# Moving a pool of streamed tiles to the other end of SBUF, in a decoder trunk on one core

## The chip, the cores and the metric

The kernel runs on one NeuronCore of a Trainium2 chip, as one launch. The metric is the device time of an execution in microseconds (us); three executions of the kernel before the change took 1943.15, 1944.34 and 1944.63 us, median 1944.34 us.

## The reference, cut to what matters

A trunk of two residual layers works on 256 tokens of width 1024. Each layer has a mixer and then an expert network with 16384 single-neuron experts. Every token picks, in 8 heads, 16 experts each, out of 128 x 128 product keys:

```python
def peer_ffn(h, w_q, sub_keys, u, v):
    ...
    def one_chunk(args):
        hc, ec, gc = args
        act = jax.nn.gelu(jnp.einsum('td,ted->te', hc, u[ec]).astype(f32), approximate=False)
        return jnp.einsum('te,ted->td', (gc * act).astype(v.dtype), v[ec])
```

`u` and `v` are 16384 x 1024 tables in float32.

## The kernel before, in words

The kernel gathers nothing. For each layer it streams both tables whole, in slabs of 128 experts (128 slabs of `u`, 128 of `v`, 512 KB each, two layers), computes every expert for every token, and masks with the gates.

A float32 product is made of three products of a reduced type: each operand is split into a rounded part `hi` and a rest `lo`. The helper `split` (L131) does it: a copy on ScalarE (ACT) writes `hi`, a subtraction on VectorE (DVE) writes `lo`. On TensorE (PE) each matrix product has a *stationary* operand, loaded by LDWEIGHTS (PEld in the profile), and a *moving* operand that streams past it.

**First product** (`u_pair`, `u_slab`). A slab of `uT` lands in a tile `raw`, is split into `hi` and `lo` (two buffers each), and 24 matmuls follow: 16 on L626 with `hi` stationary, 8 on L628 with `lo` stationary. The moving operand is always `hT`, the normalized activations (256 columns, one token a column). The first half of a layer's slabs runs beside the choice of the experts (`choose`, on DVE, in an order fixed by `in_order("DVE")`); in the second half, after every two slabs, `g_batch` makes gates of eight tokens with 16 small matmuls (L649).

**Second product** (`v_pair`, `v_acts`, `v_slab`). For two slabs the masked activations `act` are split into `whi` and `wlo` (two buffers each). A slab of `v` lands in `raw` and is split into `hi` and `lo`. Then 12 matmuls on L783 follow, with `whi` or `wlo` stationary and `hi` or `lo` moving, 512 columns each. The last six slabs of a layer run at L736.

**Where the tiles lie.** A pool takes a piece of SBUF of the same address range in all 128 partitions: from the bottom upward, or with `side="right"` from the top downward. A pool opened later lies behind the ones that are open on its side. `base` and `h` (with `hT`) are opened first at the bottom; then `st`, with `raw` (3 buffers), `hi` and `lo` (2 each); above it come the pools of the stage. At the top lie the weights of the projections (pool `wp`, with tiles that are also tagged `whi` and `wlo`) and later some activations. `whi` and `wlo` of the second product are in the pool `oh`, at the bottom above `st`.

The other user of such matmuls that the text needs is `proj_t` and `proj_n` (lines L135 to L137 by way of `mm3`), which multiply `hT` (or another tile of activations) by weights from the pool `wp`: in `proj_t` the weights are stationary, in `proj_n` they move.

Of the kernel before, what the change touches and what calls it, by code (L numbers as in the profile page):

```python
# [10 lines left out]
F32R = mybir.dt.float32r  # L11
# [8 lines left out]
P = 128  # L20
D = 1024
KD = D // P
S = 256
# [4 lines left out]
NK = 128  # L28
# [39 lines left out]
class Trunk:  # L68
# [222 lines left out]
    def tail(self, products, add, nxt, tmp):  # L291


        def run(g):
            for _ in g:
                pass
        run(products(0, 0))
        run(products(0, 1))
        run(add(0, 0))
        run(add(0, 1))  # L300
        nxt.norm(0)
        run(products(1, 0))
        p = products(1, 1)
        next(p)
        squares = add(1, 0)
        next(squares)
        nxt.turn(0)
        run(p)
        nxt.make(0, tmp, squares)
        run(add(1, 1))  # L310
# [351 lines left out]
    def peer(self, layer, e, first, right, early, middle, after, nxt, ss):  # L662

        st = self.st
        nb = S // GB
        left = ExitStack()
        dp = left.enter_context(self.pool(f"dst{layer}"))
        dst = self.t(dp, [P, 4, S], HF)  # L670
        with self.pool(f"topk{layer}") as tk:
            self.topk_consts(tk)
            mods = self.mods_in(tk, 3, *early)
            sc = [self.t(tk, [P, 16, NK]) for _ in range(TT)]
            with self.pool(f"q{layer}") as qp:
                self.queries(qp, layer, e, first, sc, mods)
            right.close()
            act0 = self.act_tiles(right.enter_context(self.pool(f"act0_{layer}", side="right")))
            chosen = self.choose(tk, sc, dst)
            with self.in_order("DVE"):  # L680
                for q in range(0, HALF, 2):
                    self.u_pair(st, layer, q, e.hT, act0, chosen)
                    if q % 4:
                        next(mods, None)
                for c in (chosen, mods):
                    for _ in c:
                        pass
        mods = self.mods_in(left.enter_context(self.pool(f"mm{layer}")), 2, *middle) if middle else iter(())
        oh = left.enter_context(self.pool(f"oh{layer}"))
        a1 = left.enter_context(self.pool(f"act1_{layer}"))  # L690
        act1 = self.act_tiles(a1)
        self.iota_t = self.t(oh, [P, NK, 2], HF)
        self.nc.gpsimd.iota(self.iota_t, pattern=[[1, NK], [0, 2]], base=0, channel_multiplier=0,
                            allow_small_or_imprecise_dtypes=True)
        done = 0
        for q in range(0, HALF, 2):
            self.u_pair(st, layer, HALF + q, e.hT, act1)
            if q % 4:
                next(mods, None)
            while done < nb and done * (HALF - 4) < nb * (q + 2):  # L700
                self.g_batch(oh, dst, act0, 0, done * GB)
                done += 1
        for _ in mods:
            pass
        accs = [[self.ps("o") for _ in range(2)] for _ in range(TT)]
        done = 0
        for q in range(0, HALF, 2):
            self.v_pair(oh, layer, q, act0, accs, q == 0)
            while q % 4 == 2 and done < nb and done * (HALF - 4) < nb * (q + 2):
                self.g_batch(oh, dst, act1, 1, done * GB)  # L710
                done += 1
        right.close()
        mods, ready = after()
        late = self.t(a1, [P, 4, 2, D], F32R, tag="act")
        nv = 6
        vs = []
        for q in range(0, HALF - nv, 2):
            self.v_pair(oh, layer, HALF + q, act1, accs, False)
            if q % 4:
                next(mods, None)  # L720
            if 34 <= q < 50 and q % 4 == 2:
                n = len(vs)
                vs.append(self.v_slab(layer, NK - nv + n, late[:, n, 0], late[:, n, 1]))
        for _ in mods:
            pass
        self.row_of(self.gate, self.modc[layer][:, 40:48])
        self.begin_order()
        ready()
        ws = [self.v_acts(oh, NK - nv + q, act1, *(("ohA", "ohA") if q == 2 else ("whi", "wlo"))) for q in (0, 2, 4)]
        vs += [self.v_slab(layer, NK - 2 + n, *self.v_parts()) for n in range(2)]  # L730

        def products(i, c):
            for m in range(0, nv, 2):
                for a, b in ((0, 0), (1, 0), (0, 1)):
                    for n in (m, m + 1):
                        self.nc.tensor.matmul(accs[i][c], ws[n // 2][a][:, n % 2, i * P:(i + 1) * P],  # L736
                                              vs[n][b][:, c * 512:(c + 1) * 512], start=False,
                                              stop=n == nv - 1 and b == 1)
                if not m:
                    yield  # L740

        def add(i, c):
            yield from self.add_gated(lambda: self.t(oh, [P, 256], tag="ohB", bufs=2), self.gate, i, c, accs[i][c], ss)
            nxt.added(i, c)
        self.tail(products, add, nxt, lambda: self.t(oh, [P, 512], tag="ohG", bufs=2))
        left.close()
# [22 lines left out]
        return [self.t(self.st, [P, D], F32R, tag=t, bufs=2) for t in ("hi", "lo")]  # L769

    def v_acts(self, pool, i2, act, *tags):
        hi, lo = (self.t(pool, [P, 2, S], F32R, tag=t, bufs=2) for t in tags or ("whi", "wlo"))
        self.split(hi, lo, self.act_of(act, i2))
        return hi, lo

# [865 lines left out]
    def run(self, out):  # L1641
        nc = self.nc
        self.hp = self.ctx.enter_context(self.pool("h"))
        self.st = self.ctx.enter_context(self.pool("st"))
        right, late = ExitStack(), ExitStack()
        self.order = ExitStack()
        start = ExitStack()
# [243 lines left out]
```

## Time and profile before

| what | value |
|---|---|
| median of three executions | 1944.34 us (1943.15 to 1944.63) |
| the profiled execution | 1942.01 us |
| its span, first to last instruction | 1940.2 us |
| PE busy | 1908.1 us, 98% of the span |
| DVE busy | 1534.9 us, 79% |
| ACT busy | 952.7 us, 49% |
| first product (L626, L628) | 4096 + 2048 matmuls |
| second product (L783) | 2928 matmuls |

The times that the text works out refer to the profiled execution, which lies 2.3 us under the median. A matmul's own duration in the profile is its way through the array; matmuls overlap, so that the distance from one start to the next is what a stream of them costs. That distance is read from a timeline: the difference of two starts, divided by the matmuls between them.

### The profile page before, as it was taken

The page shows a single profiled execution, that of the slowest core. Times are in us where ns is not written, and L with a number is a line of the kernel's source. Part 1 is how long each engine was busy: PE and PEld are TensorE (multiplying, and loading weights), DVE is VectorE, ACT ScalarE, POOL GpSimd, SP SyncE. Part 2 cuts the span into 40 slices and gives each one's busy share as a digit, 9 for nine tenths or more (in the row PEclk, how much of TensorE's full clock was granted, in tenths as well). Part 3 has the DMA queues.
Part 4 walks back from the last instruction along what each step waited for, and adds up shares of the span by engine and source line. Part 5 has one row for each costly group of instructions (what it writes and reads, how often), then busy time and mean ns, then how long its engine had stood idle before and what let it go on. Part 6 is the DMA issues. An engine that isn't in the chain of part 4 may idle for free.

```text
span 1940.2 us, 36008 instructions
## 1 busy us (share of the span) xinstructions
PE 1908.1 (98%) x14368; PEld 1753.0 (90%) x14368; DVE 1534.9 (79%) x3265; ACT 952.7 (49%) x1309; POOL 49.9 (3%) x131
## 2 busy tenths in 40 slices
PE   6999999999999999999999999999999999999998
PEld 6999999999999888888889899999999988888886
DVE  7879699989977789877657668898777778985565
ACT  3866545454344444445546664545444444444453
POOL 7000000000000000000000000000000000000000
PEclk9999999999999999999999999999999999999999
DMA  7557485558645555589743454555545555556673
GB/s 319 177 172 250 187 275 179 185 187 291 229 164 167 172 175 174 178 286 331 229 129 115 163 218 169 183 187 178 171 164 169 168 174 175 173 176 204 192 224 106
DMA packets 97080, 376.67 MB, mean 194 GB/s; under 512 B 11920, under 2 KB 12176, under 8 KB 90256
## 3 DMA queue, kind: packets, MB, share of 16 engines
q1 hardware_dynamic: 96912, 374.37, 57.4%
q8 instruction: 112, 1.84, 0.4%
q14 instruction: 56, 0.46, 0.1%
HBM read 373.28 MB, written 1.05 MB: 193 GB/s over the span
## 4 chain that ended last, share of the span: by engine, by line
PE 88%; DVE 4%; DMA 3%; ACT 2%; issue 1%; SPq 0%; ACTq 0%; DVEq 0%
PE ps L783 31%; PE ps L626 26%; PE ps L628 13%; PE ps L649 3%; PE ps L135 3%; PE ps L136 3%; PE ps L137 3%; DMA raw<-in_v_dram 2%; PE ps L736 1%; PE ps L323 1%; DVE wlo L131 1%; PE ps L1207 1%; DMA wraw<-in_w_dram 1%; PE ps L946 1%; PE ps L456 1%
## 5 line engine op out<-in xcount | busy, mean ns | idle before, releaser
L131 ACT CAST hi<-raw 128x1024 fp32r<-128x1024 f32 x508 | 533.6, 1051 | 772.6 <-PE ps L626 385.4
L131 DVE TENSOR_TENSOR lo<-raw,hi 128x1024 fp32r<-128x1024 f32 x508 | 619.8, 1221 | 260.7 <-ACT hi L131 256.7
L626 PE MATMUL ps<-hT,hi 128*128 128x256 f32 x4096 | 538.3, 284 | 0.0
L626 PEld LDWEIGHTS ps<-hT,hi 128*128 128x128 f32 x4096 | 509.0, 192 | 0.0
L628 PE MATMUL ps<-hT,lo 128*128 128x256 f32 x2048 | 287.2, 283 | 0.0
L783 PE MATMUL ps<-hi,whi 128*128 128x512 f32 x976 | 266.4, 394 | 2.0 <-ACT hi L131 1.9
L628 PEld LDWEIGHTS ps<-hT,lo 128*128 128x128 f32 x2048 | 264.2, 192 | 0.0
L783 PE MATMUL ps<-hi,wlo 128*128 128x512 f32 x976 | 261.3, 389 | 0.0
L783 PE MATMUL ps<-lo,whi 128*128 128x512 f32 x976 | 261.2, 389 | 0.0
L783 PEld LDWEIGHTS ps<-hi,wlo 128*128 128x128 f32 x976 | 183.2, 188 | 38.8
L783 PEld LDWEIGHTS ps<-lo,whi 128*128 128x128 f32 x976 | 183.1, 188 | 38.9 <-DVE lo L131 0.2
L783 PEld LDWEIGHTS ps<-hi,whi 128*128 128x128 f32 x976 | 180.1, 188 | 39.3 <-ACT hi L131 4.5
L131 DVE TENSOR_TENSOR wlo<-wraw,whi 128x1024 fp32r<-128x1024 f32 (+1 forms) x84 | 98.7, 1200 | 41.0 <-ACT whi L131 41.0
L131 ACT CAST whi<-wraw 128x1024 fp32r<-128x1024 f32 (+1 forms) x84 | 83.7, 1031 | 30.7 <-PE ps L137 9.3
L645 DVE TENSOR_TENSOR ohG<-ohB,t 128x512 f16<-128x512 f16 x256 | 98.6, 416 | 0.0
L135 PE MATMUL ps<-hT,whi 128*128 128x256 f32 x288 | 84.0, 292 | 7.7 <-ACT hT L246 7.1
L639 DVE TENSOR_TENSOR ohA<-t,t 128x1024 f16<-128x1024 f16 x128 | 87.3, 682 | 0.0
L136 PE MATMUL ps<-hT,whi 128*128 128x256 f32 x288 | 82.1, 285 | 0.2 <-DVE hT L250 0.2
L137 PE MATMUL ps<-hT,wlo 128*128 128x256 f32 x288 | 82.2, 286 | 0.0
L649 PE MATMUL ps<-ohG,ohA 128*128 128x64 f16 x2048 | 78.6, 193 | 0.0
L649 PEld LDWEIGHTS <-ohA 128*128 128x128 f16 x2048 | 67.0, 97 | 12.1 <-issue 8.5
L353 DVE SCALAR_TENSOR_TENSOR t<-t 128x1024 f32<-128x1024 f32 x56 | 67.4, 1219 | 12.6 <-DMA t<-in_modT_dram 9.5
(480 smaller groups left out, 2254.6 us busy)
## 6 DMA issues: line engine op xcount, KB each, us to landing
raw<-in_uT_dram SPq DMA_DIRECT2D x256, 512.0 KB, 3.3
raw<-in_v_dram SPq DMA_DIRECT2D x256, 512.0 KB, 3.8
t<-in_modT_dram SPq DMA_DIRECT2D x56, 512.0 KB, 5.3
wraw<-in_w_dram SPq DMA_DIRECT2D x13, 1024.0 KB, 5.9
raw<-in_modT_dram SPq DMA_DIRECT2D x24, 512.0 KB, 4.4
wraw<-in_wq_dram SPq DMA_DIRECT2D x12, 1024.0 KB, 5.9
mw<-in_mod_dram SPq DMA_DIRECT2D x8, 1024.0 KB, 13.8
wraw<-in_w0start_dram SPq DMA_DIRECT2D x4, 1024.0 KB, 12.0
```

Source lines behind the costliest of these rows:

```text
L131: return self.nc.scalar.copy(hi, src), self.nc.vector.tensor_sub(lo, src, hi.bitcast(F32))
L135: mm(out, l[0], r[0], start=start, stop=False)
L136: mm(out, l[0], r[1], start=False, stop=False)
L137: mm(out, l[1], r[0], start=False, stop=stop)
L323: mm(ps[g][:, i], e.hT[:, s, k, sl], w[:, b, k, :], start=s + k + b == 0, stop=s == 1 and n == KD - 1)
L353: self.nc.vector.scalar_tensor_tensor(w, w, 1.0, row, op0=OP.mult, op1=OP.mult, accum_out=self.modc[layer][:, c:c + 1])
L626: mm(pair, hi[:, k], hT[:, s, k], start=k == 0 and s == 0, stop=False)
L628: mm(pair, lo[:, k], hT[:, 0, k], start=False, stop=k == KD - 1)
L639: nc.vector.tensor_tensor(A, self.iota_t[:, None].to_broadcast(full), pairs(0, full), op=OP.is_equal)
L645: nc.vector.tensor_tensor(B[:, j], b0, pairs(2 + j, part), op=OP.mult)
L649: nc.tensor.matmul(ps[:, t], A[:, t // 2, :, t % 2], B[:, j, t // 2, :, t % 2], start=j == 0, stop=j == 1)
L783: self.nc.tensor.matmul(acc[i][c], w[a][:, j, i * P:(i + 1) * P], v[b][:, c * 512:(c + 1) * 512], start=first and j + a + b == 0, stop=False)
```

## The change

The pool `st` is opened at the top of SBUF (`side="right"`) instead of the bottom. The activations' parts of the second product, `whi` and `wlo`, leave the pool `oh` and go into `st` under the tags `vwh` and `vwl`; only one pair of the last six slabs keeps its place in `oh` (the tag `ohA`).

```diff
-        ws = [self.v_acts(oh, NK - nv + q, act1, *(("ohA", "ohA") if q == 2 else ("whi", "wlo"))) for q in (0, 2, 4)]
+        ws = [self.v_acts(oh, NK - nv + q, act1, *(("ohA", "ohA") if q == 2 else ())) for q in (0, 2, 4)]
...
     def v_acts(self, pool, i2, act, *tags):
-        hi, lo = (self.t(pool, [P, 2, S], F32R, tag=t, bufs=2) for t in tags or ("whi", "wlo"))
+        hi, lo = (self.t(pool if tags else self.st, [P, 2, S], F32R, tag=t, bufs=2) for t in tags or ("vwh", "vwl"))
         self.split(hi, lo, self.act_of(act, i2))
         return hi, lo
...
         self.hp = self.ctx.enter_context(self.pool("h"))
-        self.st = self.ctx.enter_context(self.pool("st"))
+        self.st = self.ctx.enter_context(self.pool("st", side="right"))
```

The instructions, their order on every engine, and the semaphores and counts that each waits for are the same in both programs. What differs is a name here and there and the addresses. On ACT, at the change from the first to the second product of layer 0, the difference reads as follows (`hi` is a slab's high part, `act` the masked activations, the number a buffer's):

```order
 L131 CAST hi_8249<-raw_8247 128x1024
 L766 ACTIVATE t_5489<-ps_8126 128x512
-L131 CAST whi_8347<-act_3027 128x512
-L131 CAST whi_8387<-act_3027 128x512
+L131 CAST vwh_8347<-act_3027 128x512
+L131 CAST vwh_8387<-act_3027 128x512
 L131 CAST hi_8281<-raw_8279 128x1024
 L131 CAST hi_8311<-raw_8309 128x1024
```

Nothing has moved: the same two casts stand at the same place, with another tag. SP, which issues the transfers, has no difference at all.

The first byte of some tiles in each partition, as the allocation of the two programs gives it, with its remainder by 128 bytes in brackets:

| tile | role | before | after |
|---|---|---|---|
| `hT` | moves in the first product | 13984 (32) | 13984 (32) |
| `hi` (two buffers) | stationary in the first product, moves in the second | 50848, 54944 (32) | 212960, 217056 (96) |
| `lo` (two buffers) | the same | 42656, 46752 (32) | 204768, 208864 (96) |
| `whi`/`vwh`, layer 0 | stationary in the second product | 84128, 86176 (32) | 221152, 223200 (96) |
| `wlo`/`vwl`, layer 0 | the same | 88224, 90272 (32) | 225248, 227296 (96) |
| `whi`, `wlo` of the projections | pool `wp` | 180192 to 229343 (96) | 143328 to 192479 (96) |
| `qkT` of the first mixer | stationary there | 93856 (32) | 65184 (32) |
| `qn` of the second mixer | stationary there | 83136 (64) | 54464 (64) |

All pools that stay at the bottom lie 28672 bytes lower after the change, all others at the top 36864 bytes lower; both are multiples of 128, so their remainders stay. Only the tiles of `st`, and with them `vwh` and `vwl`, have another remainder.

## Rows read from the trace of the kernel before

**Rows 1.** The page: busy time, and the chain that ended last.

```profile
PE 1908.1 (98%) x14368; PEld 1753.0 (90%) x14368; DVE 1534.9 (79%) x3265; ACT 952.7 (49%) x1309; POOL 49.9 (3%) x131
...
PE 88%; DVE 4%; DMA 3%; ACT 2%; issue 1%; SPq 0%; ACTq 0%; DVEq 0%
```

**Rows 2.** Groups of instructions: line, engine, names, shapes, count | busy us, mean ns | idle.

```profile
L626 PE MATMUL ps<-hT,hi 128*128 128x256 f32 x4096 | 538.3, 284 | 0.0
...
L628 PE MATMUL ps<-hT,lo 128*128 128x256 f32 x2048 | 287.2, 283 | 0.0
L783 PE MATMUL ps<-hi,whi 128*128 128x512 f32 x976 | 266.4, 394 | 2.0 <-ACT hi L131 1.9
```

**Rows 3.** PE's timeline, first product: start us, us, line, operation, count.

```profile
382.59 2.08 PE L626 MATMUL ps<-hT,hi 128*128 128x256 f32 x16
384.51 1.12 PE L628 MATMUL ps<-hT,lo 128*128 128x256 f32 x8
385.47 2.08 PE L626 MATMUL ps<-hT,hi 128*128 128x256 f32 x16
387.39 1.12 PE L628 MATMUL ps<-hT,lo 128*128 128x256 f32 x8
388.35 2.08 PE L626 MATMUL ps<-hT,hi 128*128 128x256 f32 x16
```

**Rows 4.** PE's timeline, projections with stationary weights: 36 matmuls between the rows.

```profile
240.92 0.28 PE L135 MATMUL ps<-hT,whi 128*128 128x256 f32 x1
...
245.00 0.28 PE L135 MATMUL ps<-hT,whi 128*128 128x256 f32 x1
```

**Rows 5.** The same, 20 us earlier: 27 matmuls between the rows.

```profile
219.81 0.28 PE L135 MATMUL ps<-hT,whi 128*128 128x256 f32 x1
...
222.99 0.28 PE L135 MATMUL ps<-hT,whi 128*128 128x256 f32 x1
```

**Rows 6.** Three stretches: length, PE, PEld, DVE, ACT, POOL busy, granted clock, DMA.

```profile
219.80:223.00 3.20, 3.20 (x30) 3.20 (x29) 2.45 (x3) 2.71 (x4) 0.00 (x0) 1.00 1.01 410
240.90:245.00 4.10, 4.10 (x38) 4.10 (x37) 2.80 (x3) 2.21 (x3) 0.00 (x0) 1.00 0.96 384
382.00:389.00 7.00, 7.00 (x61) 7.00 (x60) 6.16 (x28) 3.85 (x5) 0.00 (x0) 1.00 0.58 186
```

**Rows 7.** PE's timeline, second product of layer 1: 20 matmuls between the rows.

```profile
1880.43 1.07 PE L783 MATMUL ps<-hi,whi 128*128 128x512 f32 x4
...
1884.96 1.07 PE L783 MATMUL ps<-lo,whi 128*128 128x512 f32 x4
```

**Rows 8.** PE's timeline, moving weights over `qkT`: 18 matmuls between the rows.

```profile
184.27 0.39 PE L135 MATMUL ps<-whi,qkT 128*128 128x512 f32 x1
...
188.39 0.39 PE L135 MATMUL ps<-whi,qkT 128*128 128x512 f32 x1
```

**Rows 9.** PE's timeline, moving weights over `qn`: 18 matmuls between the rows.

```profile
1109.20 0.39 PE L135 MATMUL ps<-whi,qn 128*128 128x512 f32 x1
...
1113.40 0.39 PE L135 MATMUL ps<-whi,qn 128*128 128x512 f32 x1
```

**Rows 10.** Stretches of the first product: length, PE, PEld, DVE, ACT, POOL busy, clock, DMA.

```profile
262.00:300.00 38.00, 38.00 (x319) 38.00 (x318) 37.41 (x145) 18.73 (x23) 0.00 (x0) 1.00 0.70 233
300.00:347.00 47.00, 47.00 (x394) 47.00 (x394) 43.24 (x130) 23.74 (x28) 1.53 (x1) 1.00 0.56 183
349.00:400.00 51.00, 51.00 (x428) 51.00 (x427) 48.54 (x223) 22.80 (x26) 0.00 (x0) 1.00 0.54 180
...
454.00:500.00 46.00, 46.00 (x464) 45.70 (x463) 46.00 (x86) 18.73 (x22) 0.00 (x0) 1.00 0.83 281
...
1264.00:1300.00 36.00, 36.00 (x302) 36.00 (x302) 34.32 (x143) 16.69 (x19) 0.00 (x0) 1.00 0.54 180
...
1368.00:1450.00 82.00, 82.00 (x832) 81.44 (x831) 62.72 (x110) 33.87 (x39) 0.00 (x0) 1.00 0.50 166
```

**Rows 11.** PE's timeline, first product's second half: one round of two slabs and gates.

```profile
497.28 2.16 PE L626 MATMUL ps<-hT,hi 128*128 128x256 f32 x16
...
503.61 1.56 PE L626 MATMUL ps<-hT,hi 128*128 128x256 f32 x11
```

**Rows 12.** Waits between 262 and 652 us: who waited for whom, us, times, longest.

```profile
ACT hi L131 <- PE ps L626: 184.9, 111, 2.4
...
DVE lo L131 <- ACT hi L131: 43.7, 41, 1.9
ACT hi L131 <- DMA raw<-in_uT_dram: 14.4, 7, 2.5
```

## The prediction, as it was recorded before the result was known

> **What bounds the kernel now.** I read the page first: PE is busy for 98% of the span, and 88% of the chain that ended last is PE [rows 1]. The reader is to see there that neither a wait nor a transfer is to be won; time can only come from the rate at which PE runs its stream. The groups of instructions give the size of the two streams: 6144 matmuls of 256 columns in the first product, none with idle time before it, and 2928 of 512 columns in the second (976 for each of three products of parts, of which one row stands for all) [rows 2]. Then I looked at PE's timeline for the distance from start to start. In the first product two slabs take 388.35 - 382.59 = 5.76 us for 48 matmuls, 120.0 ns each [rows 3]. In the projections, where `hT` moves over weights of the pool `wp`, a matmul of the same shape follows the last after 4.08 / 36 = 113.3 ns [rows 4]; a little earlier, with the same operands from the same kind of tiles, after 3.18 / 27 = 117.8 ns [rows 5]. The granted clock is 1.00 in each of these stretches [rows 6], the full 2.4 GHz, so the three spacings are not the clock's.
>
> What differs between [rows 3] and [rows 4] is the place of the stationary operand. `hT` has remainder 32 by 128 bytes in both. In [rows 3] `hi` and `lo` also have remainder 32, and lie at the bottom like `hT`; in [rows 4, 5] the weights have remainder 96, and lie at the top. The change gives the first product the placement of [rows 4, 5].
>
> **The change, part by part.** No instruction, wait or transfer is added, removed or moved, and no queue is passed by anything, so every term is a count times a difference of spacings.
>
> *First product.* 6144 matmuls. If they run like [rows 4], each saves 120.0 - 113.3 = 6.67 ns: 41.0 us. If they run like [rows 5], 120.0 - 117.8 = 2.2 ns: 13.5 us. I take [rows 4]: a spacing settles within some matmuls after a break in the stream and then stays, and the last projections before the first product, which begins right behind them, run at that of [rows 4]. Both values stay for the range.
>
> *What is late next.* DVE makes every `lo`. It waits for ACT, and ACT for PE to give a buffer back [rows 12]; so today PE paces it. With PE at 113.3 / 120.0 = 94.4% of its time per slab, DVE must not need more. In 262 to 300 us it needs 37.41 us where PE would take 35.9: 1.5 us are lost. In 349 to 400 it needs 48.54 against 48.2: 0.4 us. In 1264 to 1300, 34.32 against 34.0: 0.3 us [rows 10]. From 454 to 500 DVE is busy without a pause; a round of 48 matmuls takes 503.61 - 497.28 = 6.33 us there [rows 11], so 46 us hold some 350 of them, whose 2.3 us are all lost. In the other stretches, such as 300 to 347 (43.24 against 44.4) or 1368 to 1450 (62.72 of 82), DVE has room [rows 10]. Together 4.5 us. At the spacing of [rows 5] PE would need 98% of its time, and DVE hardly costs anything. Transfers: 14.4 us of ACT's waits are for slabs not yet landed [rows 12]; PE waits for none of it now, and at 5% more speed I leave it at nothing; if that cover goes, the few longest (up to 2.5 us each, 7 in all) are the price, which the range takes in.
>
> *Second product.* 2928 matmuls at 4.53 / 20 = 226.5 ns [rows 7]. Here both operands move together, from remainder 32 and the bottom to remainder 96 and the top. No row has both operands at the top, or both at remainder 96, so I bound it. Above: weights of remainder 96 moving over a stationary tile at the bottom take 4.12 / 18 = 228.9 ns over `qkT` [rows 8] and 4.20 / 18 = 233.3 ns over `qn` [rows 9]: +2.4 to +6.8 ns, 7 to 20 us slower. Below: if a high place alone were what helps, the 6.67 ns of [rows 4] against [rows 3], 20 us faster. I take zero, because the relation of the two operands, equal remainders and the same end, is that of [rows 7].
>
> *The rest.* `first_queries` also puts weights into `hi` and `lo`, and the last six slabs mix both places; some hundred matmuls with a few ns each, in both directions: nothing. The pools that only slide keep their remainders and their end.
>
> Sum: 41.0 - 4.5 = 36.5 us off the profiled execution's 1942.0 us gives 1905.5; the median stands 2.3 us above that execution, hence **1908 us**.
>
> **A rule that speaks against it.** The rows show three spacings for one shape and one clock. The Trainium skill, page "SBUF — State Buffer", section "SBUF: two separate sides", says that contention arises only at the port pair that GpSimd and VectorE share, or at the transfer side, and that TensorE never waits on anyone; page "TensorE: Matmul & The Clock Gate", part 2, adds that loading the next weights takes no read bandwidth from the running matmul. By these the place of a tile would cost nothing and the sum would be 0, with the time at 1944. The trace agrees badly: [rows 3] and [rows 4] differ by 6.67 ns with nothing else changed that I can name.
>
> **The rivals.**
> 1. *The slower of the two spacings.* The first product settles at that of [rows 5]. For it: the same kinds of tiles ran at both. Against it: [rows 4] are the nearer in time to the first product. 1944.3 - 13.5 = 1931 us.
> 2. *The place decides nothing.* The 120 ns come from how the first product is fed (ACT and DVE write `hi` and `lo` while PE reads), not from addresses. For it: [rows 4, 5] differ with the same tiles, so something besides place acts. Against it: the first three stretches of [rows 10] have 119 ns of PE's time per matmul alike (38.00 / 319, 47.00 / 394, 51.00 / 428, a matmul at either edge counted in), with DVE busy for 98, 92 and 95% of them. 1944 us. (The two pages of the Trainium skill named above would have this one.)
> 3. *The moving operand's own place decides, and a high one is slow* (the slower side). `hT` does not move, so the first product keeps 120 ns; in the second `hi` and `lo` now move from remainder 96 like the weights of [rows 8, 9]. For it: those rows are the slowest of the 512-column kind. Against it: [rows 3, 4] have the same `hT`. Its price is 7 us at 228.9 ns and 20 us at 233.3: 1951 to 1964 us. With the first product unchanged it decides as soon as the second goes over 226.5 by 1.3 ns (3.9 us over 2928 matmuls).
>
> **How the numbers follow.** Forecast 65%, with 1902 to 1918 of its own (from no loss on DVE, 1903, to some stretches at the spacing of [rows 5]); rival 1 20%; rival 2 8%; rival 3 7%. About 0.2% (3.9 us) is what a measurement of this kernel can tell from no change. Faster: 65 + 20 = 0.85; same 0.08; slower 0.07. The range must leave out no more than 2 in 10: from 1902 to 1932 it holds the forecast and rival 1 (0.85, less a little for their own edges), and part of the case in which the first product gains in full and the second loses up to 20 us.
>
> **What would show it.** In the profile after, PE's timeline of the first product should read 2.72 us for 24 matmuls where it now reads 2.88, and the duration of one matmul on L626 should fall from 283 or 284 ns to about 276; L783 should keep its spacing of 226.5 ns. The span of each first product should shrink by some 20 us in layer 1 and 16 in layer 0, where DVE's stretches without a pause lie, and waits of PE for `lo` should appear in those. Wrong it is if L626 keeps 120 ns, if L783 goes above 228 ns, or if PE's new waits for `lo` or for landed slabs go well beyond 5 us.

## The result, and the profile after

The changed kernel takes **1913.42 us**, the median of four executions (1911.78 to 1916.04); the kernel before, in four executions, takes 1944.49 us. The ratio is 0.9843, 95% interval 0.9826 to 0.986. The change is faster, as forecast, and lies 5 us above the predicted 1908 us and inside the range. The profiled execution went from 1942.01 to 1913.79 us: 28.2 us, where the sum said 36.5.

The page after, busy time and the chain that ended last; the lines answer to [rows 1]:

```profile
PE 1875.2 (98%) x14368; PEld 1716.0 (90%) x14368; DVE 1532.6 (80%) x3265; ACT 951.4 (50%) x1309; POOL 51.4 (3%) x131
...
PE 77%; DVE 10%; DMA 7%; ACT 4%; issue 2%; SPq 0%; ACTq 0%; DVEq 0%
```

The same 14368 matmuls keep PE busy for 33 us less. In the chain PE has given 11% of the span to the others, DVE (6%) and the transfers (4%) above all: PE still bounds the kernel, but no longer alone. The groups of instructions (busy us, mean ns of one | idle before), which answer to [rows 2]:

```profile
L626 PE MATMUL ps<-hT,hi 128*128 128x256 f32 x4096 | 513.1, 278 | 2.0 <-ACT hi L131 2.0
...
L628 PE MATMUL ps<-hT,lo 128*128 128x256 f32 x2048 | 275.7, 277 | 1.3 <-DVE lo L131 1.2
L783 PE MATMUL ps<-hi,vwh 128*128 128x512 f32 x976 | 266.5, 394 | 2.9 <-ACT hi L131 2.6
```

The gain is in the first two rows: a matmul of the first product falls from 284 and 283 ns to 278 and 277, L783 stays at 394, and small idle times stand behind the bars where [rows 2] has 0.0 for the first product. PE's timeline in the first product (start us, us, engine, line, operation, count), as in [rows 3]:

```profile
382.38 1.98 PE L626 MATMUL ps<-hT,hi 128*128 128x256 f32 x16
384.19 1.07 PE L628 MATMUL ps<-hT,lo 128*128 128x256 f32 x8
385.10 1.98 PE L626 MATMUL ps<-hT,hi 128*128 128x256 f32 x16
```

24 matmuls take 385.10 - 382.38 = 2.72 us, 113.3 ns each, the predicted figure to the digit. The second product, as in [rows 7]:

```profile
1879.83 1.07 PE L783 MATMUL ps<-hi,vwh 128*128 128x512 f32 x4
...
1884.37 1.07 PE L783 MATMUL ps<-lo,vwh 128*128 128x512 f32 x4
```

20 matmuls in 4.54 us: 227 ns, unchanged.

To add up a whole product, the distance from the start of each of its matmuls to the start of PE's next one was taken. A distance of at most 25 ns above 256 or 512 columns at 2.4 GHz (106.7 or 213.3 ns) counts as part of a stream, whose mean is its *spacing*; what longer distances have beyond this mean is the *loss at breaks*. "Span" is from the first start to the last end.

| | before | after |
|---|---|---|
| first product, spacing of 6144 matmuls | 119.98 ns | 113.71 ns |
| first product, loss at breaks | 5.3 us | 12.1 us |
| second product (L783), spacing | 227.3 ns | 227.2 ns |
| second product, loss at breaks | 6.8 us | 9.7 us |
| span of the first product, layer 0 and 1 | 387.5, 387.5 us | 374.7, 368.9 us |
| span of the second product, layer 0 and 1 | 352.8, 351.1 us | 356.0, 350.7 us |

The faster spacing gives 6144 x 6.27 = 38.5 us; new breaks take back 12.1 - 5.3 = 6.8 us in the first product and 9.7 - 6.8 = 2.9 us in the second: 28.8 us, against 28.2 measured. Nearly all of the new breaks are in layer 0 (6.4 of the 6.8 us), whose first product won 12.8 us where layer 1's won 18.6; forecast were 16 and 20.

The breaks in the trace. Stretches of the changed kernel (length, then PE, PEld, DVE, ACT and POOL busy, granted clock, DMA share, GB/s), as in [rows 10]:

```profile
262.00:300.00 38.00, 38.00 (x338) 38.00 (x337) 37.72 (x147) 20.09 (x25) 0.00 (x0) 1.00 0.71 235
300.00:347.00 47.00, 46.76 (x407) 46.24 (x406) 44.99 (x141) 24.40 (x29) 1.53 (x1) 1.00 0.56 189
454.00:500.00 46.00, 44.76 (x462) 43.68 (x461) 46.00 (x84) 18.53 (x21) 0.00 (x0) 1.00 0.81 278
```

In 454 to 500 DVE has no pause and PE stands still for 1.24 us, mostly in waits for `lo` of up to 0.5 us, as predicted. It gets through 462 matmuls there, where [rows 10] has 464, so the faster spacing wins nothing in this stretch: counted from start to start, the loss at breaks is 3.0 us against 0.6 before. PE's idle time shows only a part of such a loss. In 262 to 300 PE loses nothing (338 matmuls for 319), where 1.5 us were predicted. In 300 to 347, where room was predicted, it is idle for 0.24 us and loses 1.2 us from start to start. The largest single break is elsewhere, on ACT (ACT's timeline, then PE's next matmul, with the idle time and its releaser):

```profile
433.25 1.28 ACT L349 ACT_TABLE_LOAD   x1 [3.81 <-DMA t<-in_cond_dram]
434.55 1.06 ACT L349 ACTIVATE t<-t 128x1024 f32<-128x1024 f32 x1
435.51 1.03 ACT L131 CAST hi<-raw 128x1024 fp32r<-128x1024 f32 x1
```

```profile
436.59 0.61 PE L626 MATMUL ps<-hT,hi 128*128 128x256 f32 x3 [1.89 <-ACT hi L131]
```

At the start of layer 0's second half `mods_in` makes its row of conditions on ACT. ACT waits 3.81 us for the row, and the next slab's `hi` is queued behind it. Before, the same wait was 1.5 us and PE had no idle time for it; now the break costs PE 2.1 us from start to start.

### The profile page after: what moved, and what is told of

The parts are those of the page before. It is cut to its first block, busy times and chain, and to the rows that moved or that the text cites. A ratio compares the mean times of both kernels' runs of the same rounds, so it can differ in the third digit from the quotient of the medians.

```text
span 1912.0 us, 36008 instructions
## 1 busy us (share of the span) xinstructions
PE 1875.2 (98%) x14368; PEld 1716.0 (90%) x14368; DVE 1532.6 (80%) x3265; ACT 951.4 (50%) x1309; POOL 51.4 (3%) x131
## 4 chain that ended last, share of the span: by engine, by line
PE 77%; DVE 10%; DMA 7%; ACT 4%; issue 2%; SPq 0%; ACTq 0%; DVEq 0%
PE ps L783 26%; PE ps L626 21%; PE ps L628 11%; DMA raw<-in_v_dram 4%; DVE lo L131 3%; PE ps L649 3%; PE ps L135 3%; PE ps L137 3%; PE ps L136 3%; DMA t<-in_modT_dram 2%; PE ps L736 1%; ACT hi L131 1%; DVE t L353 1%; PE ps L323 1%; PE ps L1207 1%
## 5 line engine op out<-in xcount | busy, mean ns | idle before, releaser
L131 ACT CAST hi<-raw 128x1024 fp32r<-128x1024 f32 x508 | 534.4, 1054 | 741.8 <-PE ps L626 301.1
L131 DVE TENSOR_TENSOR lo<-raw,hi 128x1024 fp32r<-128x1024 f32 x508 | 619.2, 1221 | 233.6 <-ACT hi L131 231.0
L626 PE MATMUL ps<-hT,hi 128*128 128x256 f32 x4096 | 513.1, 278 | 2.0 <-ACT hi L131 2.0
L626 PEld LDWEIGHTS ps<-hT,hi 128*128 128x128 f32 x4096 | 484.6, 188 | 2.5 <-ACT hi L131 2.4
L628 PE MATMUL ps<-hT,lo 128*128 128x256 f32 x2048 | 275.7, 277 | 1.3 <-DVE lo L131 1.2
L783 PE MATMUL ps<-hi,vwh 128*128 128x512 f32 x976 | 266.5, 394 | 2.9 <-ACT hi L131 2.6
L783 PE MATMUL ps<-lo,vwh 128*128 128x512 f32 x976 | 261.8, 390 | 0.4 <-DVE lo L131 0.3
L783 PE MATMUL ps<-hi,vwl 128*128 128x512 f32 x976 | 261.3, 389 | 0.0
L628 PEld LDWEIGHTS ps<-hT,lo 128*128 128x128 f32 x2048 | 251.9, 188 | 2.6 <-DVE lo L131 2.3
L783 PEld LDWEIGHTS ps<-lo,vwh 128*128 128x128 f32 x976 | 182.6, 188 | 40.5 <-DVE lo L131 2.8
L783 PEld LDWEIGHTS ps<-hi,vwl 128*128 128x128 f32 x976 | 183.2, 188 | 38.9
L783 PEld LDWEIGHTS ps<-hi,vwh 128*128 128x128 f32 x976 | 180.1, 188 | 40.8 <-ACT hi L131 5.7
L131 DVE TENSOR_TENSOR wlo<-wraw,whi 128x1024 fp32r<-128x1024 f32 (+1 forms) x84 | 99.1, 1203 | 40.3 <-ACT whi L131 40.3
L131 ACT CAST whi<-wraw 128x1024 fp32r<-128x1024 f32 (+1 forms) x84 | 83.7, 1032 | 29.8 <-PE ps L137 8.7
L353 DVE SCALAR_TENSOR_TENSOR t<-t 128x1024 f32<-128x1024 f32 x56 | 67.3, 1220 | 17.8 <-DMA t<-in_modT_dram 12.2
```

What stands on the lines that cost most here:

```text
L131: return self.nc.scalar.copy(hi, src), self.nc.vector.tensor_sub(lo, src, hi.bitcast(F32))
L353: self.nc.vector.scalar_tensor_tensor(w, w, 1.0, row, op0=OP.mult, op1=OP.mult, accum_out=self.modc[layer][:, c:c + 1])
L626: mm(pair, hi[:, k], hT[:, s, k], start=k == 0 and s == 0, stop=False)
L628: mm(pair, lo[:, k], hT[:, 0, k], start=False, stop=k == KD - 1)
L783: self.nc.tensor.matmul(acc[i][c], w[a][:, j, i * P:(i + 1) * P], v[b][:, c * 512:(c + 1) * 512], start=first and j + a + b == 0, stop=False)
```

## The experiments

Each ratio in this part is to the kernel before, in executions taken beside it (medians of 1944.5 to 1946.2 us).

In the addresses of the two programs, two things differ. One is the end of SBUF. The other is where the tiles start modulo 256 bytes, and with it **the start of the stationary operand less the start of the moving one, modulo 256** (called the *relation* below). `hT` starts at 160 (modulo 256) in both. Before, `hi`, `lo`, `whi` and `wlo` of the products start at 160 too: relation 0 in both products. After, all of `st` starts at 224: relation 64 in the first product, 0 in the second. So the theory "the end of SBUF decides" and the theory "the relation decides" fit the result equally, and the first four kernels separate them, and the two halves of the change.

### The old end with the new relation, and the new end with the old one

The pool goes back to the bottom, between two paddings of together 256 bytes:

```diff
-        self.st = self.ctx.enter_context(self.pool("st", side="right"))
+        self.t(self.ctx.enter_context(self.pool("pad0")), [P, 16], tag="pad0")
+        self.st = self.ctx.enter_context(self.pool("st"))
+        self.t(self.ctx.enter_context(self.pool("pad1")), [P, 48], tag="pad1")
```

> Only addresses differ from the kernel after: the pool of the streamed tiles is back at the bottom, but 64 bytes higher, so that hi and lo have remainder 96 by 128 bytes and hT keeps 32; the parts of the second product are in that pool and share its remainder. Theory A, the remainders of the two operands decide: the first product keeps the spacing of after, 113 to 114 ns, and the time is that of after, about 1913 us. Theory B, the end of SBUF decides (stationary at the top, moving at the bottom): the first product is at 120.0 ns again and the time about 1944 us.

And the pool at the top, but 64 bytes lower:

```diff
+        self.t(self.ctx.enter_context(self.pool("pad0", side="right")), [P, 16], tag="pad0")
         self.st = self.ctx.enter_context(self.pool("st", side="right"))
+        self.t(self.ctx.enter_context(self.pool("pad1", side="right")), [P, 48], tag="pad1")
```

> Only addresses differ from the kernel after: the pool is at the top, but 64 bytes lower, so that hi, lo, vwh and vwl have remainder 32 like hT. Theory A, the remainders decide: the first product runs at 120.0 ns and the time is about 1944 us, as before. Theory B, the end of SBUF decides: 113 to 114 ns and about 1913 us.

At the bottom with relation 64 the kernel takes 1915.26 us, ratio 0.984 (0.982 to 0.986), with a spacing of 114.0 ns. At the top with relation 0 it takes 1946.39 us, ratio 1.0001 (0.999 to 1.0013), with 119.98 ns. The groups of these two kernels, in this order:

```profile
L626 PE MATMUL ps<-hT,hi 128*128 128x256 f32 x4096 | 514.1, 278 | 1.8 <-ACT hi L131 1.8
```

```profile
L626 PE MATMUL ps<-hT,hi 128*128 128x256 f32 x4096 | 538.4, 284 | 0.0
```

The first agrees with the row of after (513.1 us, 278 ns), the second with that of before (538.3 us, 284 ns). The end of SBUF makes no difference in either; a shift of 64 bytes carries the whole gain. That 256 bytes are enough to reckon by shows here too: the `hi` of the changed kernel and of the one at the bottom with relation 64 lie 162048 bytes apart, 633 times 256; by 512 bytes their relations would differ, and their spacings agree (113.7 and 114.0 ns).

### Each half of the change

Only the pool moves; `whi` and `wlo` stay in `oh` (relation 64 in the first product, 192 in the second). The edit is on the kernel before:

```diff
-        self.st = self.ctx.enter_context(self.pool("st"))
+        self.st = self.ctx.enter_context(self.pool("st", side="right"))
```

> One part of the change alone: the pool goes to the top, whi and wlo of the second product stay in their pool at the bottom with remainder 32, so that in the second product a moving operand of remainder 96 meets a stationary one of 32, as when weights moved over qkT (228.9 ns) or near to the case over qn (233.3 ns). Theory A: the first product as after (113 to 114 ns), the second at 229 to 233 instead of 226.7 ns, 7 to 20 us slower than after: 1920 to 1933 us. Rival: the second product does not mind where its operands lie, 226.7 ns and about 1913 us.

And `vwh` and `vwl` move into a pool of their own at the top, so that the first product keeps 64 and the second gets 64 as well (an edit on the changed kernel, as are all that follow):

```diff
-        hi, lo = (self.t(pool if tags else self.st, [P, 2, S], F32R, tag=t, bufs=2) for t in tags or ("vwh", "vwl"))
+        hi, lo = (self.t(pool if tags else self.vw, [P, 2, S], F32R, tag=t, bufs=2) for t in tags or ("vwh", "vwl"))
...
+        self.t(self.ctx.enter_context(self.pool("pad0", side="right")), [P, 48], tag="pad0")
+        self.vw = self.ctx.enter_context(self.pool("vw", side="right"))
+        self.t(self.ctx.enter_context(self.pool("pad1", side="right")), [P, 16], tag="pad1")
         self.st = self.ctx.enter_context(self.pool("st", side="right"))
```

> The pool of the change, with vwh and vwl 64 bytes above it by remainder: in the second product the stationary operand now stands to the moving one as hi does to hT in the first product after the change (64 bytes more, by 256). Theory A in its simplest form, that this relation is the fast one for any width: the second product falls from 226.7 to about 220 ns, 20 us off, about 1894 us. Rival: at 512 columns the loading of weights is hidden anyway, and the relation can only be as good as equal remainders or worse: 226.7 to 233 ns, 1913 to 1933 us.

The pool alone: 1918.58 us, ratio 0.9863 (0.9846 to 0.9879), second product at 229.1 ns (as expected; the time lies 1.4 us under the range expected). The second product at relation 64: 1927.28 us, ratio 0.9917 (0.9897 to 0.9936), at 233.3 ns. PE's timeline of the latter shows the price at the place of [rows 7]:

```profile
1880.41 1.09 PE L783 MATMUL ps<-hi,vwl 128*128 128x512 f32 x4
...
1885.08 1.10 PE L783 MATMUL ps<-hi,vwh 128*128 128x512 f32 x4
```

20 matmuls take 4.67 us, 233.5 ns. The spacing of 233.3 makes 2928 x 6.1 = 18 us more than at 227.2, of which the breaks, 6.8 us smaller in this run, hide some. The same relation that speeds up the first product slows the second. So the second part of the change, `whi` and `wlo` into the pool, has nothing to win, since the second product had relation 0 already: it keeps 1.8 ns a matmul (5 us) from being lost. The spacing shows this; the ratios of the pool alone and of the whole change overlap in their intervals.

### Many relations in one run

Larger slots put the two buffers of a tag on different remainders. The first kernel (`vw` is used as above; the second adds a padding of 32 bytes at the top and one of 224 bytes below `st`):

```diff
+        self.vw = self.ctx.enter_context(self.pool("vw", side="right"))
         self.st = self.ctx.enter_context(self.pool("st", side="right"))
+        for tag in ("hi", "lo"):
+            self.t(self.st, [P, D + 16], F32R, tag=tag, bufs=2)
+        for tag in ("vwh", "vwl"):
+            self.t(self.vw, [P, 512 + 32], F32R, tag=tag, bufs=2)
```

> As the changed kernel, but every buffer of hi and lo lies 64 bytes, and every buffer of vwh and vwl 128 bytes, further on in its slot, so that one run shows several relations (start of the stationary operand less that of the moving one, modulo 256). First product: 64 and 128 for hi, 192 and 0 for lo. Second product: 0, 64, 128 and 192 mixed from buffer to buffer. Theory: only the relation counts, with a period of 256: 0 costs 120.0 ns at 256 columns, 64 costs 113.3, 128 and 192 something between 113 and 118; at 512 columns 0 costs 226.7, 192 costs 229, 64 costs 233. Rival: the period is 128, so that hi's buffer at 128 costs 120.0 as 0 does. Second rival: what counts is that all of a stream has one relation, and mixing them costs 120 or more everywhere.

> As the run before with all of the pool 32 bytes lower: first product 32 and 96 for hi, 160 and 224 for lo; second product multiples of 64 again. Theory: none of the four is equal, so none costs 120.0; all lie at 113 to 118 ns. Rival: 32-byte steps count like their 64-byte neighbour below (32 as 0: 120.0 ns). If any is under 113.3 ns, there is a better place than the change's.

They take 1940.7 and 1945.3 us, in one execution each. Sorted by relation, the spacing in the first product is 119.5 (0), 118.2 (32), 116.2 (64), 117.6 (96), 118.6 (128), 119.7 (160), 117.9 (192) and 117.0 ns (224). The period of 128 is out: 64 and 192 differ, and so do 0 and 128. But "only 0 is dear" is out too, with 118 to 120 ns at 32, 128 and 160; and 64 is dearer here than in a stream of its own. In the second product every relation costs 230 to 233 ns, also 0. A stream that changes its relation every 4 to 16 matmuls doesn't show each price cleanly, so the next kernels keep one relation throughout.

### One relation throughout: 128, 224, and 32

Three paddings, here for 128 in both products; for 224 they are 32, 56 and 40 words:

```diff
+        self.t(self.ctx.enter_context(self.pool("pad0", side="right")), [P, 16], tag="pad0")
+        self.vw = self.ctx.enter_context(self.pool("vw", side="right"))
+        self.t(self.ctx.enter_context(self.pool("pad1", side="right")), [P, 32], tag="pad1")
         self.st = self.ctx.enter_context(self.pool("st", side="right"))
+        self.t(self.ctx.enter_context(self.pool("pad2", side="right")), [P, 16], tag="pad2")
```

> As the changed kernel, with paddings at the top so that all buffers of hi and lo have the relation 128 to hT in the first product, and all of vwh and vwl the relation 128 to hi and lo in the second. The two spread kernels gave 117.9 and 118.1 ns a matmul of the first product for every relation, also for 64, which alone in a stream costs 113.7; so a stream has to keep one relation to show its own price. Theory (a period of 256, equal is worst at 256 columns): 114 to 118 ns in the first product, 227 to 233 in the second. Rival (a period of 128): 120.0 and 226.7 ns. Under 113.3 or 226.7 would be a better place than the change's.

> The same with the relation 224 in both products. Theory (only equal starts cost 120.0): 113 to 118 ns in the first product; in the second, where a few matmuls with relation 224 took 233 ns, about 233. Rival (32-byte steps count like a neighbour of 64: 0 or 192): 120.0 or 117.7 ns, and 226.7 or 229. Under 113.3 or 226.7 would be a better place than the change's.

And relation 64 in the first product with 32 in the second (56 words above `vw`, 8 below):

> The changed kernel's relation 64 in the first product, and the relation 32 in the second (vwh and vwl in a pool of their own at the top, with paddings). Of the second product's relations kept through a whole kernel 0 cost 227.2 ns a matmul, 192 cost 229.1, 128 cost 232.7, 64 and 224 cost 233.3. Theory: equal starts are the best there, so 32 lies between 228 and 233 ns, the second product is 2 to 18 us longer over its 2928 matmuls, and the time is 1915 to 1931 us. Rival: small offsets beat equal starts as 64 does in the first product; then it is under 226 ns and the time under 1910 us.

The first two, in one execution each, take 1951.2 and 1946.9 us, no better than before; the third takes 1927.89 us, ratio 0.9908 (0.989 to 0.9925). All kernels that keep one relation, together:

| relation | first product, ns | second product, ns |
|---|---|---|
| 0 | 120.0 | 227.2 to 227.3 |
| 32 | | 233.3 |
| 64 | 113.7 to 114.1 | 233.3 |
| 128 | 118.7 | 232.7 |
| 192 | | 229.1 |
| 224 | 117.2 | 233.3 |

(The expectation of the kernel with 128 says of the spread kernels that every relation cost 117.9 to 118.1; that was the mean over their relations.) Both rivals on a better place fall: of the six relations tried in the second product 0 is the cheapest, of the four in the first 64. For the other four of the first product the spread kernels show 117.6 to 119.7 ns; as they also show 116.2 for 64, a better one among these is unlikely, but not excluded. The change hit the best pair that was found.

One rival is left in the first product: `hT` never moves there, so the stationary operand's own start changes together with the relation. In the second product the two come apart: with the stationary operand at 160 (modulo 256), a matmul takes 227.3 ns when the moving one is at 160 (the kernel before), 229.1 at 224 (the pool alone) and 232.7 at 32 (relation 128). At 256 columns, projections of the kernel before do the same on a small scale. There weights at 224 move over `hT` at 160, relation 192 (PE's timeline, 20 matmuls between the rows):

```profile
162.80 0.28 PE L136 MATMUL ps<-wlo,hT 128*128 128x256 f32 x1
...
165.15 0.28 PE L135 MATMUL ps<-whi,hT 128*128 128x256 f32 x1
```

That is 117.5 ns, where the first product of the same kernel takes 120.0 with its stationary operand at 160 too. So the start of the stationary operand alone does not decide. The cheap relation itself, 64 at 256 columns, was kept throughout with one pair of starts only, 224 over 160.

### Where the rest of the expected gain went

Layer 0's second half of the first product holds 16 sums for layer 1's modulation (L353 on DVE, 1.22 us each, with 512 KB to load); layer 1 has none there. The first kernel moves them into the second product's second half, the second leaves them out, with the row of conditions:

```diff
             self.u_pair(st, layer, HALF + q, e.hT, act1)
-            if q % 4:
-                next(mods, None)
...
-        mods, ready = after()
+        mid, (mods, ready) = mods, after()
...
             if q % 4:
                 next(mods, None)
+            else:
+                with self.tc.issue_after(self.lead.ins), self.tc.issue_after(self.tail_of.ins):
+                    next(mid, None)
```

(`mid` makes the sums; `lead` and `tail_of` are the load and the subtraction of the last slab, behind which each of them is held.)

> On top of the changed kernel, the 16 modulation sums of layer 1 (L353 on DVE, with their 512 KB loads) that run in layer 0's second half of the first product go into the second half of the second product, behind the split of every second pair of slabs. DVE is busy 57.9 of 60.0 us at 440 to 500 there, and the first product of layer 0 is 374.4 us long where layer 1's, which has no such sums in its second half, is 368.6. Theory: those 5.8 us are DVE and its loads being late next; the first product of layer 0 then comes to 369 to 371 us and the waits for ACT's hi and DVE's lo in 430 to 500 us go. The second product's second half had a DMA share of 0.75 and takes 8 MB more: between nothing (about 1909 us) and as much as was won (1914). Rival: the breaks come from the stream of PE itself (the way it starts again), then layer 0 stays at 374 and the time at 1913 or above.

```diff
-        self.peer(0, e1, first, right, ((0, 5), (1, 0)), ((1, 1), (1, 2)), before_mla, e2, self.ss2)
+        nc.vector.memset(self.modc[1][:, 8:24], 0.0)
...
+        self.peer(0, e1, first, right, ((0, 5), (1, 0)), (), before_mla, e2, self.ss2)
```

> The changed kernel without these 16 sums and their loads at all (two columns of layer 1's modulation are zeros instead, so that part of the computation is left out). Theory: layer 0's first product is 369 to 371 us, the second as before, and the time 1908 to 1910 us. Rival: layer 0's first product stays within 1 us of 374.4 and the time within 1.5 us of 1913.4.

Left out: layer 0's first product takes 369.7 us instead of 374.7, the time is 1912.43 us, ratio 0.9821 (0.9805 to 0.9838). The span is as the theory had it; the median is 2 us over its bound, where the rival had it (within 1.5 us of 1913.4), and the executions scatter from 1908.47 to 1913.5. In the profiled one, 1912.97 us, the granted clock falls ahead of all that was left out, behind a wait of PE for ACT of 0.74 us (length, PE, PEld, DVE, ACT and POOL busy, granted clock, DMA share, GB/s):

```profile
64.00:72.00 8.00, 7.74 (x39) 7.72 (x40) 6.71 (x26) 6.17 (x10) 0.00 (x0) 0.57 0.85 303
```

So the first product begins 2.5 us later than in the changed kernel's profile, where the clock is 1.00 there, and half of the gain is hidden: the span carries this finding and the time does not. Moved: layer 0's first product takes 371.1 us, but its second 366.3 instead of 356.0, and the time is 1917.06 us (ratio 0.9848, 0.9832 to 0.9865), 3 us over the theory's bound. What was won is given back: by the ratios this kernel and the change cannot be told apart. The stretch of the second product into which the sums went:

```profile
820.00:1002.00 182.00, 173.29 (x741) 140.56 (x740) 137.09 (x167) 89.50 (x103) 0.00 (x0) 0.97 0.85 298
```

PE stands still for 8.7 of 182 us, in four waits for `hi` of 8.0 us together (the longest 3.4 us), at a DMA share of 0.85. At the two longest the granted clock falls to half: its mean is 0.76 over 930 to 937 us and 0.72 over 958 to 970 (PE's timeline at the first):

```profile
932.89 1.77 PE L783 MATMUL ps<-hi,vwh 128*128 128x512 f32 x4 [3.37 <-ACT hi L131]
934.46 1.91 PE L783 MATMUL ps<-hi,vwl 128*128 128x512 f32 x4
936.17 1.31 PE L783 MATMUL ps<-lo,vwh 128*128 128x512 f32 x4
937.32 1.07 PE L783 MATMUL ps<-hi,vwh 128*128 128x512 f32 x4
```

Four matmuls take 1.91 us there instead of 1.07. This profiled execution lies 8 us over its median, so the size is not to be taken from it.

The last of the kernels spreads the sums thinly: twelve over the rest of the first product's second half and four over the first half of the second product.

```diff
+    def behind(self, mods):
+        with self.tc.issue_after(self.lead[0].ins), self.tc.issue_after(self.lead[1].ins):
+            next(mods, None)
...
-            if q % 4:
-                next(mods, None)
+            if q > 16 and q % 4:
+                self.behind(mods)
...
             self.v_pair(oh, layer, q, act0, accs, q == 0)
+            if q and not q % 8:
+                self.behind(mods)
```

> On top of the changed kernel, layer 0's 16 sums of the second half of the first product are spread: none before the tenth pair of slabs, then one after every second pair, each held behind the split of the slab before it, and the rest in the first half of the second product, one in every fourth pair. Leaving the sums out made layer 0's first product 369.7 us instead of 374.7; moving them into the second product's later half made it 371.1 but the second product 366.3 instead of 356.0. Theory: spread thin they cost at most 1 us, layer 0's first product is 369 to 371 us, its second stays at 355 to 357 and the time is 1908 to 1911 us. Rival: DVE has no room anywhere (182 of 187 us busy in this half by its parts), then the lost 4 to 5 us only move, and the time stays at 1912 to 1915.

It takes **1909.89 us** (five executions, 1909.16 to 1914.19), ratio 0.9822 (0.9808 to 0.9836): the lowest median of all kernels that compute everything. Layer 0's first product takes 371.0 us, its second 353.9. The interval overlaps that of the change, so that the 3.5 us between the medians are supported by the spans (374.7 and 356.0 us in the change) rather than by the times. The stretch 446 to 500 us, of the changed kernel and of this one:

```profile
446.00:500.00 54.00, 52.46 (x539) 51.09 (x536) 52.63 (x95) 22.19 (x26) 0.00 (x0) 1.00 0.82 283
```

```profile
446.00:500.00 54.00, 54.00 (x576) 53.67 (x574) 44.84 (x81) 23.12 (x27) 0.00 (x0) 1.00 0.53 182
```

With DVE at 44.84 us instead of 52.63 and the DMA share at 0.53 instead of 0.82, PE has no pause. The rest of the first product is now fuller, and PE's waits between 261 and 632 us are down to two:

```profile
PE ps L628 <- DVE lo L131: 0.5, 1, 0.5
PE ps L626 <- ACT hi L131: 0.2, 1, 0.2
```

The rival, that DVE has no room anywhere and the loss only moves, falls.

## Why the prediction was right, and where it was off

*What bounds the kernel.* Right: PE's spacing, at a granted clock of 1.00 before and after; the gain came from it alone.

*First product, 41.0 us.* Right in kind and nearly in size: 38.5 us. The choice of [rows 4] over [rows 5] was right for most of the stream, but both occur: of 6055 distances some 450 are 117 to 119 ns, two thirds of them in layer 1, and at 4 to 5 ns each they make most of the 2.5 us that are missing. The step "a spacing settles within some matmuls after a break and then stays" holds for both, and a break can change from one to the other. For example (PE's timeline of the changed kernel):

```profile
321.99 1.98 PE L626 MATMUL ps<-hT,hi 128*128 128x256 f32 x16
323.88 1.19 PE L628 MATMUL ps<-hT,lo 128*128 128x256 f32 x8
324.91 1.98 PE L626 MATMUL ps<-hT,hi 128*128 128x256 f32 x16
326.72 1.07 PE L628 MATMUL ps<-hT,lo 128*128 128x256 f32 x8
```

16 matmuls from 321.99 to 323.88 take 118 ns each, 16 from 324.91 to 326.72 take 113. What selects one was not found. The reason given for [rows 4], that the last projections run at it, reaches no further than the first break; that the stream took the faster one after most of the others too was partly luck.

*"What differs is the place of the stationary operand."* Right in the remainder, wrong in naming the end of SBUF beside it, and too narrow: it is the start of one operand against that of the other, and by 256 bytes, not by the 128 of the table of addresses: by 128 the relations 0 and 128 would be one, and they took 120.0 and 118.7 ns, 227.2 and 232.7. By it the rows that bounded the second product fit: weights at 224 over `qkT` at 160 have relation 192 and 228.9 ns [rows 8], over `qn` at 192 relation 224 and 233.3 ns [rows 9], and whole second products at these relations took 229.1 and 233.3. [Rows 4, 5] both have 64.

*What is late next, 4.5 us.* Mis-sized, and made up otherwise: 6.8 us in the first product. Its largest term came out: of 454 to 500 all of the gain is lost, 2.4 us more at breaks than before, where 2.3 were predicted. The 1.5 us of 262 to 300, the 0.4 of 349 to 400 and the 0.3 of 1264 to 1300 did not come: PE has no idle time there, though DVE is busy for 37.72 of the first 38.00 us. The step that failed is to take DVE's busy time in a stretch for the need of the slabs that PE uses up in it. Of 262 to 300 in the kernel before, the line of L131 alone reads (length, DVE and ACT busy, granted clock, DMA share, GB/s):

```profile
262.00:300.00 38.00, 16.53 (x14) 13.84 (x14) 1.00 0.70 233
```

16.53 us at 1.22 us each are some 13.5 slabs, where PE used up 38.00 / 2.88 = 13.2: a part of DVE's time went into slabs to come. That nothing at all was lost is not explained by this alone, and was not tested. What was left out are the single wait of ACT for the row of conditions, which cost 2.1 us, and the 1.2 us of 300 to 347. The transfers' cover shrank too: ACT's waits for slabs are 14.4 us in [rows 12] and 48.6 us after (261 to 636 us), nearly all hidden still:

```profile
ACT hi L131 <- PE ps L626: 126.5, 81, 2.3
...
ACT hi L131 <- DMA raw<-in_uT_dram: 48.6, 25, 3.6
```

*Second product, 0.* Right for the spacing, and for the reason given (the relation stays that of [rows 7]; the end of SBUF, named beside it, had no part). But layer 0's was 3.2 us longer by new breaks; a cause for them was not tested. In both layers the breaks cost 2.9 us more, and with the 2.5 and 2.3 us above these are 7.7 of the 8.3 us between the sum and the measured gain.

*Rivals.* Rival 1 (1931 us) occurs in patches only. Rival 2 (the place decides nothing) is refuted by a shift of 64 bytes that undoes the whole gain: 120.0 against 113.7 ns at the same feed and clock. The Trainium skill, page "SBUF — State Buffer", section "SBUF: two separate sides", says that TensorE never waits on anyone; what the prediction drew from it, that a tile's place costs nothing, does not hold here, and whether TensorE waits at a port no run shows. Rival 3 (the moving operand's own place) is refuted by `hT`, which didn't move, and by the second product, whose moving operand went to 224 at no cost; its two prices are those of the relations 192 and 224, which the second product would have had from other remainders.

## What to carry to other kernels

Where matmuls follow each other without a gap and PE bounds the kernel, read the start-to-start distance from the timeline, and if two streams of one shape and clock differ, compare the starts of the stationary and the moving operand modulo 256 bytes; a padding of 64 bytes was worth 1.6% here. Measure it for each shape apart, since relation 64 was the best for 256 columns and among the worst for 512. After such a gain look for the engine that had just enough time before, and spread its side work thinly instead of where there is room on average.

## What the hardware showed that was not expected

- Spacing depends on the relation of the two operands' addresses, not on the stationary one's alone or on the end of SBUF: 113.7 to 120.0 ns at 256 columns, 227.2 to 233.3 ns at 512, in streams at a granted clock of 1.00.
- At 256 columns the weight load shows it as well: its mean on L626 is 192 ns before and 188 after, on L783 188 in both (PEld's group of the changed kernel):

```profile
L626 PEld LDWEIGHTS ps<-hT,hi 128*128 128x128 f32 x4096 | 484.6, 188 | 2.5 <-ACT hi L131 2.4
```

- One relation, 64, has two lasting spacings at 256 columns, 113.3 and about 117.7 ns, and a stream can change between them at a break. Why stays open, as does the mechanism behind the relation itself: the runs show its prices only.
